# Operand splitting and block sums of a fast matrix product, moved from GpSimd to VectorE and put in another order

## The chip, the cores and the metric

The kernel runs on one core of a Trainium2 chip. Its engines are TensorE (PE in the rows, with its weight loads as PEld), VectorE (DVE), ScalarE (ACT), GpSimd (POOL) and SyncE (SP), which here issues the DMAs. The metric is the device time of one execution in microseconds, the median of three runs.

## The reference, cut to what matters

Two trunk layers act on 512 latent tokens and 128 context tokens, 640 rows of width 1024. Each layer has attention and then a SwiGLU feed-forward block of hidden width 2816. All is float32. What the change touches is the first half of the feed-forward block:

```
h = rms_norm(x, norm_ffn) * (1.0 + sc_f) + sh_f
gate, up = jnp.split(h @ w_gate_up, 2, axis=-1)
x = x + g_f * ((jax.nn.silu(gate) * up) @ w_down)
```

## The kernel before, in words

Every large matrix product is made of three matmuls. An operand is kept as a high part (the value rounded by a ScalarE copy to the fast matmul type) and a low part (the value minus its high part), and `prod` adds high·high, low·high and high·low in PSUM. `split` (L82) makes both parts: ScalarE writes the high one (L87), VectorE the low one (L88). Weights arrive by DMA as `raw` tiles, 1 MB each, two buffers, and are split into `whi` and `wlo`, four buffers of each.

In layer 1 (`FAST`) the gate and up products use the Strassen-Winograd scheme: the hidden activation, 1024 x 640, is cut into four blocks B11, B21 (first 320 tokens) and B12, B22 (last 320 tokens), each of four 128x320 tiles. From them come four sums, T3 = B22 - B12, T1 = B12 - B11, T2 = B22 - T1, T4 = B21 - T2. Seven products of a weight block with one of B11, B21, T2, T3, T1, T4, B22 replace eight. The weight blocks need sums too (`fast_prep`, L499): POOL makes four per raw tile, L506 to L509.

While these operands come into being, the first unit of 256 gate and up columns is done with the plain eight products (`plain_units`, L557). Its first half (`c == 0`) multiplies B11 and B21, its second half B12 and B22. Then come the fast products, seven for each of gate and up, in the order of their weight blocks A11, A12, S2, S3, S1, A22, S4, which multiply B11, B21, T2, T3, T1, T4, B22.

Before, the operands of the second half and all four sums are split by `cut` (L440): ScalarE writes the high part (L443), and POOL, not VectorE, the low part (L444). `fast_norm` (L446) does so for B12 and B22, `fast_sums` (L481) for T3, T1, T2, T4. The sums themselves run on VectorE (L487, L490, L492, L495, L496), all of them called between the two halves of `plain_units`. The weights of the next unit are split when `w_next` asks for them, which is after the second half in program order.

The program is not run in the order of the Python code: a scheduler orders each engine's queue by its own estimate of time, and each engine then works through its queue in order. An instruction that waits holds up all that is behind it on its engine. The names in the rows that follow: `lo4`-`lo7` are the tiles of B12; `k8`, `k9`, `q0`, `q1` those of B22; `q2`-`q5` T3; `q6`, `q7` and two `Q` tiles T1; a `Q` tile and three pieces of `V` T2; four pieces of `V` T4. `hi4`-`hi7` hold the unsplit B12 and B22 and later T1 and T2; three other `Q` tiles hold T3 and T4 before their split.

Of the kernel before, what the change touches and what calls it, by code (L numbers as in the profile page):

```python
# [11 lines left out]
F32 = mybir.dt.float32  # L12
F32R = mybir.dt.float32r
I32 = mybir.dt.int32
AF = mybir.ActivationFunctionType
ALU = mybir.AluOpType
# [5 lines left out]
KC = D // P  # L22
# [24 lines left out]
class Net:  # L47
# [389 lines left out]
        h = self.temp % 2  # L437
        return self.temps[self.temp // 2][:, h * HALF:(h + 1) * HALF]

    def cut(self, pair, src):  # L440

        hi, lo = pair
        self.nc.scalar.activation(hi, src, AF.Copy)  # L443
        self.nc.gpsimd.tensor_tensor(lo, src, hi.bitcast(F32), ALU.subtract)  # L444

    def fast_norm(self, state, half, rb):  # L446

        nc = self.nc
        v = nc.vector
        l, _, T, a = state  # L450
        g0, g1 = HALVES[half]
        segs = [(s, e, c) for s, e, c in ((g0, min(g1, DEC), 0), (DEC, g1, 1)) if s < e]

        def scaled(out, k):
            for s, e, c in segs:
                v.scalar_tensor_tensor(out[:, s - g0:e - g0], self.xT[k][:, s:e], a[:, k, c:c + 1],
                                       rb[:, s - g0:e - g0], ALU.mult, ALU.mult)

        n = KC // 2
        if half == 0:  # L460
            self.whole = {}
            for name, k0 in (("B11", 0), ("B21", n)):
                for i in range(n):
                    tmp = self.t([P, HALF], "P", bufs=3)
                    scaled(tmp, k0 + i)
                    self.split(*T[name][i], tmp, bias=self.m(l, 3, k0 + i, 0))
            return
        T["B12"] = []
        for i in range(n):
            tmp = self.t([P, 2, HALF], f"hi{n + i}")  # L470
            b12 = self.t([P, NT], f"lo{n + i}", F32R)
            T["B12"].append((b12[:, 0:HALF], b12[:, HALF:NT]))
            for j, k in enumerate((i, n + i)):
                scaled(tmp[:, j], k)
                for s, e, c in segs:
                    w = tmp[:, j, s - g0:e - g0]
                    nc.scalar.activation(w, w, AF.Identity, bias=self.m(l, 3, k, c))
                self.cut(T[("B12", "B22")[j]][i], tmp[:, j])
            self.whole[i] = tmp

    def fast_sums(self, T):  # L481

        v = self.nc.vector
        for i in range(KC // 2):
            b12, b22 = self.whole[i][:, 0], self.whole[i][:, 1]
            t3 = self.fast_temp()
            v.tensor_tensor(t3, b22, b12, ALU.subtract)  # L487
            self.cut(T["T3"][i], t3)
            for part in T["B11"][i]:
                v.tensor_tensor(b12, b12, part.bitcast(F32), ALU.subtract)  # L490
            self.cut(T["T1"][i], b12)
            v.tensor_tensor(b22, b22, b12, ALU.subtract)  # L492
            self.cut(T["T2"][i], b22)
            t4 = self.fast_temp()
            v.tensor_tensor(t4, T["B21"][i][0].bitcast(F32), b22, ALU.subtract)  # L495
            v.tensor_tensor(t4, t4, T["B21"][i][1].bitcast(F32), ALU.add)  # L496
            self.cut(T["T4"][i], t4)

    def fast_prep(self, raw, name):  # L499

# [56 lines left out]
    def plain_units(self, T, act):  # L557

        nc = self.nc
        g = [self.t([P, NT], "P", bufs=3) for _ in range(2)]
        n = KC // 2
        rows = [(k, b, i) for i in range(n) for k, b in ((i, 0), (n + i, 1))]
        w = [[self.w_next(1), self.w_next(1)], [self.w_next(1), self.w_next(0)]]
        for c, names in enumerate((("B11", "B21"), ("B12", "B22"))):
            if c == 0:
                rows = sorted(rows)
            else:  # L570
                self.fast_sums(T)
                rows = sorted(rows, key=lambda x: (x[2], x[0]))
            for r in range(2):
                s = self.S()
                o = g[r][:, c * HALF:(c + 1) * HALF]
                p = s[:, 0:HALF], s[:, 512:512 + HALF]
                for u in range(2):
                    hi, lo = w[r][u]
                    self.prod(p[u], [((hi[:, k], lo[:, k]), T[names[b]][i]) for k, b, i in rows])
                    if u == 0:  # L580
                        nc.scalar.activation(o, p[0], AF.Silu)
                nc.vector.tensor_tensor(o, p[1], o, ALU.mult)
        a = act(0), act(1)
        for r in range(2):
            self.split(*a[r], g[r])
# [751 lines left out]
```

## Time and profile before

| | |
|---|---|
| median of three runs | 1721.56 us (1719.19 to 1723.73) |
| profiled execution | 1722.35 us, of it 1720.3 us span |
| mean granted TensorE clock | 0.981 |
| TensorE busy | 1657.2 us, 96% of the span |
| VectorE, ScalarE, POOL busy | 1178.0, 671.5, 457.8 us |
| instructions of L443 and L444 | 24 each, between 1283 and 1315 us |

TensorE is busy nearly all the time, so what matters is each stretch in which it waits or runs at the lower of its two clock levels. PEclk in a row is the granted clock as a share of full speed: 1.00 is 2.4 GHz and 0.50 is 1.2 GHz. A duration in the timeline is that of the record; engines overlap the end of one instruction with the next, so the cost of one in a row of many is the distance between their starts.

### The profile page before, as it was taken

Reading aid. Unit: us, or ns where it says so; the run is one execution under the profiler, and the core shown is the slowest. Engines: PE = TensorE matmul, PEld = TensorE weight load, DVE = VectorE, ACT = ScalarE, POOL = GpSimd, SP = SyncE. Lnnn points to the kernel's source line nnn. Section 1 sums busy time; section 2 is a strip of 40 time slices with the busy share of each in tenths; the row PEclk is TensorE's granted clock in tenths of the full one; section 3 lists DMA queues with packets and bytes.
Section 4 is the critical chain, followed back from the end, with each engine's and each line's share of the span. In section 5 each row is a group of like instructions: output and inputs, shape, how many; then the busy total and the mean of one; then the engine's idle time right before and its main releaser. Section 6 shows DMA issues by size and latency. Waiting matters only on the chain.

```text
span 1720.3 us, 29417 instructions
## 1 busy us (share of the span) xinstructions
PE 1657.2 (96%) x11958; PEld 1577.8 (92%) x11958; DVE 1178.0 (68%) x1999; ACT 671.5 (39%) x1301; POOL 457.8 (27%) x402
## 2 busy tenths in 40 slices
PE   8989899999999999999999998999998999999999
PEld 6868878898999999999999998888987999999998
DVE  5686768878588987732257885678479944873772
ACT  4433376643422122212235524767344422441440
POOL 0242634410100000000003354453027613741440
PEclk8989999999999999999999999999998999999999
DMA  9343211144155555312122211112211222231222
GB/s 329 137 152 117 56 25 26 50 172 147 50 193 185 183 201 189 129 60 88 62 102 74 75 38 44 26 40 67 91 50 39 85 99 74 74 103 70 74 82 79
DMA packets 44263, 169.22 MB, mean 98 GB/s; under 512 B 5600, under 2 KB 8416, under 8 KB 32864
## 3 DMA queue, kind: packets, MB, share of 16 engines
q1 hardware_dynamic: 44128, 167.34, 29.2%
q8 instruction: 94, 1.54, 0.4%
q14 instruction: 41, 0.34, 0.1%
HBM read 152.90 MB, written 3.93 MB: 91 GB/s over the span
## 4 chain that ended last, share of the span: by engine, by line
PE 84%; DVE 7%; ACT 3%; DMA 2%; POOL 2%; issue 2%; SPq 0%; POOLq 0%; DVEq 0%; ACTq 0%
PE S L712 21%; PE S L711 21%; PE S L713 21%; PE S L1006 3%; PE mm L1027 3%; PE S L922 3%; PE S L923 2%; PE mm L1023 2%; PE S L237 2%; PE mm L711 1%; PE mm L712 1%; PE mm L713 1%; DMA Q<-in_w_mod 1%; DVE wlo L88 1%; DVE mx L942 1%
## 5 line engine op out<-in xcount | busy, mean ns | idle before, releaser
L87 ACT ACTIVATE whi<-raw 128x1024 fp32r<-128x1024 f32 (+2 forms) x272 | 224.6, 842 | 617.4 <-PE S L712 526.6
L88 DVE TENSOR_TENSOR wlo<-raw,whi 128x1024 fp32r<-128x1024 f32 (+2 forms) x272 | 302.4, 1127 | 100.2 <-ACT whi L87 95.9
L711 PE MATMUL S<-k,whi 128*128 128x256 f32 (+2 forms) x904 | 277.5, 310 | 9.3 <-ACT whi L87 8.0
L713 PE MATMUL S<-k,wlo 128*128 128x256 f32 (+2 forms) x904 | 279.2, 309 | 0.0
L712 PE MATMUL S<-lo,whi 128*128 128x256 f32 (+2 forms) x880 | 272.7, 310 | 0.0
L713 PE MATMUL S<-hi,wlo 128*128 128x384 f32 (+2 forms) x864 | 266.9, 310 | 0.0
L711 PE MATMUL S<-hi,whi 128*128 128x256 f32 (+2 forms) x864 | 266.2, 310 | 0.0
L712 PE MATMUL S<-q,whi 128*128 128x256 f32 (+2 forms) x832 | 257.6, 310 | 0.4 <-POOL q L444 0.4
L1158 DVE SCALAR_TENSOR_TENSOR x<-S,modT,x 128x128 f32<-128x128 f32 (+4 forms) x137 | 66.7, 525 | 195.5 <-PE S L713 195.4
L711 PEld LDWEIGHTS S<-k,whi 128*128 128x128 f32 x904 | 170.6, 190 | 10.9 <-ACT whi L87 8.3
L713 PEld LDWEIGHTS S<-k,wlo 128*128 128x128 f32 x904 | 171.0, 189 | 0.0
L712 PEld LDWEIGHTS S<-lo,whi 128*128 128x128 f32 x880 | 165.7, 188 | 1.7 <-issue 1.7
L713 PEld LDWEIGHTS S<-hi,wlo 128*128 128x128 f32 x864 | 162.5, 188 | 0.0
L711 PEld LDWEIGHTS S<-hi,whi 128*128 128x128 f32 x864 | 161.7, 188 | 0.8 <-issue 0.8
L712 PEld LDWEIGHTS S<-q,whi 128*128 128x128 f32 x832 | 157.0, 189 | 4.1 <-issue 3.4
L629 POOL TENSOR_TENSOR lo<-P,hi 128x640 fp32r<-128x640 f32 (+2 forms) x12 | 13.3, 1107 | 533.1 <-ACT hi L628 532.7
L317 DVE SCALAR_TENSOR_TENSOR Q<-V,cT,Q 128x512 f32<-128x512 f32 x224 | 152.8, 749 | 0.0
L711 PE MATMUL S<-whi,hi 128*128 128x256 f32 x512 | 146.8, 287 | 2.4 <-ACT Q L245 1.9
L942 DVE TENSOR_REDUCE mx<-S 128x1 f32<-128x768 f32 x128 | 119.5, 951 | 42.6 <-PE S L923 42.3
L713 PE MATMUL S<-whi,lo 128*128 128x256 f32 x512 | 145.9, 286 | 0.0
L712 PE MATMUL S<-wlo,hi 128*128 128x256 f32 x512 | 145.5, 284 | 0.0
L711 PEld LDWEIGHTS S<-whi,hi 128*128 128x128 f32 x512 | 97.5, 190 | 5.5 <-issue 2.5
(272 smaller groups left out, 3657.4 us busy)
## 6 DMA issues: line engine op xcount, KB each, us to landing
raw<-in_w_gate_up SPq DMA_DIRECT2D x44, 1024.0 KB, 4.8
V<-in_w_mod SPq DMA_DIRECT2D x64, 512.0 KB, 3.9
raw<-in_w_in SPq DMA_DIRECT2D x16, 1024.0 KB, 4.9
raw<-in_w_down SPq DMA_DIRECT2D x16, 1024.0 KB, 5.0
Q<-in_w_mod SPq DMA_DIRECT2D x32, 256.0 KB, 3.7
raw<-in_w_out SPq DMA_DIRECT2D x8, 1024.0 KB, 4.8
raw<-in_w_down SPq DMA_DIRECT2D x8, 768.0 KB, 4.2
raw<-raw SPq DMA_DIRECT2D x40, 128.0 KB, 2.2
```

What stands on the lines that cost most here:

```text
L87: nc.scalar.activation(hi, src, AF.Copy)
L88: nc.vector.tensor_tensor(lo, src, hi.bitcast(F32), ALU.subtract)
L237: nc.tensor.matmul(o, lhsT=l_[k][:, c], rhs=r_[:, w], start=k == 0 and i == 0, stop=k == KC - 1 and i == 2)
L317: ins = nc.vector.scalar_tensor_tensor(a, v, self.cT[:, k, c:c + 1], a, ALU.mult, ALU.add)
L711: self.nc.tensor.matmul(out, lhsT=lh, rhs=rh, start=(i == 0), stop=False)
L712: self.nc.tensor.matmul(out, lhsT=lh, rhs=rl, start=False, stop=False)
L713: self.nc.tensor.matmul(out, lhsT=ll, rhs=rh, start=False, stop=(i == n - 1))
L922: nc.tensor.matmul(out, lhsT=Q[j][:, cols], rhs=keys[:, k0:k0 + n], start=True, stop=False)
L942: nc.vector.tensor_reduce(mx, s[:, 0:n], AX.X, ALU.max, negate=True)
L1006: nc.tensor.transpose(ps[:, i * P:(i + 1) * P], p[:, i * P:(i + 1) * P], self.ident)
L1027: nc.tensor.matmul(o[64 * j:64 * j + 64], lhsT=self.V[:, v, 512 + 64 * j:576 + 64 * j], rhs=pts[j][:, i * P:(i + 1) * P], start=first, sto ...
L1158: self.nc.vector.scalar_tensor_tensor(x[:, s:e], src[:, s - a:e - a], self.m(l, which, mb, c), x[:, s:e], ALU.mult, ALU.add)
```

## The change

`cut` is gone. Wherever it stood, `split` stands: the low parts of B12, B22, T1, T2, T3 and T4, 24 of 128x320, are now VectorE's (L88). `fast_sums` is a generator in three parts. Its first part makes T3, T1 and T2 and splits T2 and T3; its second splits T1 and makes and splits T4. The first is called between the two halves of `plain_units` as before, the second after both, and between them the split of the next unit's first weights is called (`w_prep(self.pos + 3)`: A11, A12 and S2). Nothing else is edited.

```diff
-    def cut(self, pair, src):
-
-        hi, lo = pair
-        self.nc.scalar.activation(hi, src, AF.Copy)
-        self.nc.gpsimd.tensor_tensor(lo, src, hi.bitcast(F32), ALU.subtract)
-
...
-                self.cut(T[("B12", "B22")[j]][i], tmp[:, j])
+                self.split(*T[("B12", "B22")[j]][i], tmp[:, j])
             self.whole[i] = tmp
 
     def fast_sums(self, T):
 
         v = self.nc.vector
-        for i in range(KC // 2):
+        n = KC // 2
+        for i in range(n):
+
             b12, b22 = self.whole[i][:, 0], self.whole[i][:, 1]
             t3 = self.fast_temp()
             v.tensor_tensor(t3, b22, b12, ALU.subtract)
-            self.cut(T["T3"][i], t3)
             for part in T["B11"][i]:
                 v.tensor_tensor(b12, b12, part.bitcast(F32), ALU.subtract)
-            self.cut(T["T1"][i], b12)
             v.tensor_tensor(b22, b22, b12, ALU.subtract)
-            self.cut(T["T2"][i], b22)
+            self.split(*T["T2"][i], b22)
+            self.split(*T["T3"][i], t3)
+        yield
+        for i in range(n):
+            self.split(*T["T1"][i], self.whole[i][:, 0])
+        for i in range(n):
             t4 = self.fast_temp()
-            v.tensor_tensor(t4, T["B21"][i][0].bitcast(F32), b22, ALU.subtract)
+            v.tensor_tensor(t4, T["B21"][i][0].bitcast(F32), self.whole[i][:, 1], ALU.subtract)
             v.tensor_tensor(t4, t4, T["B21"][i][1].bitcast(F32), ALU.add)
-            self.cut(T["T4"][i], t4)
+            self.split(*T["T4"][i], t4)
+        yield
...
-                self.fast_sums(T)
+                sums = self.fast_sums(T)
+                next(sums)
                 rows = sorted(rows, key=lambda x: (x[2], x[0]))
...
                 nc.vector.tensor_tensor(o, p[1], o, ALU.mult)
+        self.w_prep(self.pos + 3)
+        next(sums)
         a = act(0), act(1)
```

What the scheduler makes of it, first on ScalarE, where the high part of the first fast weight stands. Before it is `whi_13609`, behind high parts of T1, T2 and T4 (`q7`, `V`, `Q`):

```order
L443 ACTIVATE q3_12986<-Q_12995 128x320
L443 ACTIVATE q4_12987<-Q_12996 128x320
L443 ACTIVATE V_12972<-Q_12995 128x320
L443 ACTIVATE q5_12988<-Q_12994 128x320
L443 ACTIVATE q7_12990<-hi5_13284 128x320
L443 ACTIVATE V_12972<-hi5_13284 128x320
L443 ACTIVATE Q_12991<-hi6_13298 128x320
L443 ACTIVATE V_12972<-hi6_13298 128x320
L87 ACTIVATE whi_13609<-raw_13607 128x512 x2
```

In the changed kernel it is `whi_13574` (its L582 is the Silu of the plain unit, L581 before):

```order
L87 ACTIVATE q3_12986<-Q_12995 128x320
L87 ACTIVATE q4_12987<-Q_12995 128x320
L87 ACTIVATE q5_12988<-Q_12996 128x320
L87 ACTIVATE whi_13574<-raw_13572 128x512 x2
L582 ACTIVATE P_13326<-S_13470 128x320
L87 ACTIVATE whi_13585<-raw_13572 128x512
L582 ACTIVATE P_13327<-S_13521 128x320
L87 ACTIVATE V_12972<-Q_12996 128x320
L87 ACTIVATE q7_12990<-hi5_13284 128x320
```

The weight's high part now stands behind T3 alone (`q3` to `q5`), and five high parts that were ahead of it are behind it. On VectorE the end of the sums reads before as follows (the low parts are on POOL; `wlo` is a low part of a weight, L582 the product of gate and up):

```order
L88 TENSOR_TENSOR wlo_13610<-raw_13607,whi_13609 128x512
L496 TENSOR_TENSOR Q_12994<-Q_12994,k6_12979 128x320
L88 TENSOR_TENSOR wlo_13610<-raw_13607,whi_13609 128x512
L88 TENSOR_TENSOR wlo_13621<-raw_13607,whi_13620 128x512
L495 TENSOR_TENSOR Q_12995<-k7_12980,hi7_13312 128x320
L496 TENSOR_TENSOR Q_12995<-Q_12995,k7_12980 128x320
L582 TENSOR_TENSOR P_13326<-S_13494,P_13326 128x320
```

and in the changed kernel, where the three last low parts of T4 are the rows `V_12972<-Q`:

```order
L495 TENSOR_TENSOR Q_12995<-Q_12995,k7_12980 128x320
L88 TENSOR_TENSOR V_12972<-Q_12994,V_12972 128x320
L88 TENSOR_TENSOR wlo_13696<-raw_13676,whi_13695 128x512
L88 TENSOR_TENSOR V_12972<-Q_12994,V_12972 128x320
L532 TENSOR_TENSOR Q_12995<-S_13659,Q_12995 128x320
L88 TENSOR_TENSOR wlo_13737<-raw_13676,whi_13736 128x512
L88 TENSOR_TENSOR wlo_13737<-PT_13711,whi_13736 128x512
L88 TENSOR_TENSOR V_12972<-Q_12995,V_12972 128x320
```

T4's last low part now comes behind weight splits of the second fast unit. TensorE of the changed kernel uses it here (the product of A22 with T4, in `S_13694`):

```order
L714 MATMUL S_13694<-V_12972,whi_13626 128x320
L714 MATMUL mm_13864<-k8_12981,whi_13769 128x320
L715 MATMUL mm_13864<-k8_12981,whi_13769 128x320
L715 MATMUL S_13694<-V_12972,whi_13626 128x320
L716 MATMUL S_13694<-V_12972,wlo_13627 128x320
L714 MATMUL S_13788<-Q_12993,whi_13695 128x320
```

The fourth row is the one that waits for that low part, and everything behind it on TensorE waits with it. POOL loses its 24 instructions and keeps the weight sums, in the same order.

## Rows read from the trace of the kernel before

**Rows 1.** The page: busy time of the engines, then the chain's shares by engine.
```profile
PE 1657.2 (96%) x11958; PEld 1577.8 (92%) x11958; DVE 1178.0 (68%) x1999; ACT 671.5 (39%) x1301; POOL 457.8 (27%) x402
PE 84%; DVE 7%; ACT 3%; DMA 2%; POOL 2%; issue 2%; SPq 0%; POOLq 0%; DVEq 0%; ACTq 0%
```

**Rows 2.** Stages: length, busy us (instructions) by engine, granted clock, DMA share, GB/s.
```profile
1290.00:1300.00 10.00, 6.34 (x42) 5.82 (x40) 9.96 (x10) 4.01 (x10) 10.00 (x10) 0.94 0.00 1
1300.00:1310.00 10.00, 5.21 (x21) 4.87 (x22) 10.00 (x13) 5.13 (x12) 7.77 (x8) 0.54 0.01 2
```

**Rows 3.** Timeline of TensorE: start us, us, operation, [idle before, releaser].
```profile
1288.90 0.31 PE L711 MATMUL S<-lo,whi 128*128 128x320 f32 x1
1289.05 0.31 PE L712 MATMUL S<-lo,whi 128*128 128x320 f32 x1
...
1295.93 0.41 PE L712 MATMUL S<-q,whi 128*128 128x320 f32 x1 [0.44 <-POOL q L444]
1296.18 0.31 PE L713 MATMUL S<-q,wlo 128*128 128x320 f32 x1
...
1304.79 0.63 PE L711 MATMUL S<-k,whi 128*128 128x320 f32 x1 [8.01 <-ACT whi L87]
...
1308.73 0.47 PE L713 MATMUL S<-k,wlo 128*128 128x320 f32 x1
1309.00 0.37 PE L711 MATMUL S<-lo,whi 128*128 128x320 f32 x1
```

**Rows 4.** Timeline of ScalarE at the end of that stall.
```profile
1303.75 0.47 ACT L443 ACTIVATE V<-hi 128x320 fp32r<-128x320 f32 x1 [1.31 <-DVE hi L492]
1304.12 1.13 ACT L87 ACTIVATE whi<-raw 128x512 fp32r<-128x512 f32 x2
1305.16 0.42 ACT L581 ACTIVATE P<-S 128x320 f32<-128x320 f32 x1
```

**Rows 5.** Timeline of VectorE, from the first sum on.
```profile
1286.69 0.48 DVE L487 TENSOR_TENSOR Q<-hi 128x320 f32<-128x320 f32 x1
...
1302.57 1.14 DVE L492 TENSOR_TENSOR hi<-hi 128x320 f32<-128x320 f32 x1
...
1305.79 0.48 DVE L495 TENSOR_TENSOR Q<-k,hi 128x320 f32<-128x320 f32 x1
1306.19 0.48 DVE L496 TENSOR_TENSOR Q<-Q,k 128x320 f32<-128x320 f32 x1
...
1312.17 1.06 DVE L496 TENSOR_TENSOR Q<-Q,k 128x320 f32<-128x320 f32 x1
...
1317.72 1.28 DVE L88 TENSOR_TENSOR wlo<-raw,whi 128x512 fp32r<-128x512 f32 x2
1318.92 0.81 DVE L88 TENSOR_TENSOR lo<-P,hi 128x640 fp32r<-128x640 f32 x1
...
1322.81 2.27 DVE L88 TENSOR_TENSOR wlo<-raw,whi 128x512 fp32r<-128x512 f32 x2
```

**Rows 6.** Timeline of POOL in the same stretch.
```profile
1303.33 1.10 POOL L444 TENSOR_TENSOR Q<-hi,Q 128x320 fp32r<-128x320 f32 x1
1304.40 1.12 POOL L444 TENSOR_TENSOR V<-hi,V 128x320 fp32r<-128x320 f32 x1
...
1322.63 1.29 POOL L509 TENSOR_TENSOR raw<-raw 128x512 f32<-128x512 f32 x1 [1.74 <-DVE wlo L88]
```

**Rows 7.** Stages around two earlier stalls, columns as in rows 2.
```profile
1030.00:1032.00 2.00, 0.75 (x7) 0.51 (x5) 0.57 (x1) 0.39 (x1) 1.94 (x2) 1.00 0.02 5
1032.00:1034.00 2.00, 1.16 (x10) 0.93 (x9) 0.00 (x0) 0.00 (x0) 2.00 (x3) 1.00 0.00 0
1266.00:1268.00 2.00, 0.77 (x7) 0.59 (x5) 2.00 (x6) 2.00 (x5) 0.00 (x0) 1.00 0.90 360
1268.00:1270.00 2.00, 0.70 (x7) 0.48 (x5) 2.00 (x4) 0.53 (x2) 0.30 (x1) 1.00 0.32 135
...
1272.00:1274.00 2.00, 2.00 (x10) 2.00 (x8) 2.00 (x5) 0.61 (x2) 0.55 (x1) 0.50 0.63 266
```

## The prediction

> **What bounds the kernel now.** I read the page first: TensorE is busy 96% of the span and 84% of the chain [rows 1], so an edit pays only where TensorE waits or runs slow. The view by stages finds the place: from 1290 to 1310 us TensorE is busy 6.34 and 5.21 of 10 us, while VectorE shows 9.96 and 10.00 and POOL 10.00 and 7.77 [rows 2]. This is just where L443 and L444 work. The timeline of TensorE shows the loss itself [rows 3]. From 1288.90 it takes 48 matmuls of the plain unit's second half, 0.147 us apart, and would be through at 1295.94. It waits 0.44 us for a POOL low part, starts the next instruction, the first fast product with weight A11, only at 1304.79 after an idle 8.01 us, and then runs at 1.2 GHz: the granted clock is 0.54 in that stretch [rows 2] and matmuls stand 0.27 us apart until 1309.00 [rows 3]. The matmul at 1309.00 is the 15th from the one at 1304.79, so 14 distances of 0.147, 2.06 us, would have done. It would have started at 1298.00: TensorE loses 11.0 us here, and after it no view shows it waiting again before the last stores.
>
> The timeline of ScalarE says why the stall ends so late [rows 4]: A11's high part starts at 1304.12, as soon as the high part ahead of it in the queue (T2's third tile) is done, and that one waited for VectorE's sum (L492), which ends at 1303.71 [rows 5]. VectorE is not slow by its own work. Its 128x320 operations take 1.14 us while POOL works, and stand 0.40 us apart at 1305.79 and 1306.19 in a gap of POOL's [rows 5]. POOL's own stand 1.07 apart [rows 6]. The two engines take turns.
>
> The page SBUF — State Buffer of the Trainium skill (Who interferes with whom) states the same: a VectorE instruction with two SBUF inputs and a GpSimd instruction that reads SBUF exclude each other for a whole instruction. [...]
>
> **The change, part by part.**
>
> *Low parts on VectorE.* POOL loses 24 instructions and is then idle until it may overwrite the first raw tile, that is until A11's low part exists. VectorE gains 24 of a kind that no row shows: 128x320, all operands in SBUF. Nearest are the sums of that shape: 0.40 us alone, 1.07 in turns [rows 5, 6]. I take 0.40, since POOL has nothing to do there.
>
> *A11's split earlier.* In the changed queue of ScalarE A11 stands right behind T3. VectorE's last T3 sum is the 19th instruction from 1286.69, so it ends at about 1286.69 + 19 x 0.40 = 1294.3. But A11's high part overwrites the weight of the plain unit's first product, which TensorE reads until about 1295.65 (the 45th of the 48 matmuls starts at 1295.35 and takes 0.31). With a high part 0.62 us (record, two in 1.13 [rows 4]) A11 is ready at 1296.3, and TensorE, through at 1295.94, waits 0.45 us in place of 8.01. No low part is late before that: the last one of B22 is the 15th VectorE instruction, 1292.7, and is wanted at 1295.3.
>
> *What is late next.* Three things.
> - The rest of the plain unit accumulates in a PSUM tile that the Silu (0.42 us [rows 4]) must first read, and the Silu stands behind A11's and A12's high parts: TensorE waits another 0.5 us and is there at 1297.4.
> - T2's second low part is VectorE's 47th instruction (41 of 0.40, 6 weight low parts of 0.60, by the pair in 1.28 [rows 5]: 20.0 us), with two weight sums of POOL in between. Such a sum costs VectorE about 1.0 us (a pair of weight low parts takes 2.27 beside POOL's L509 and 1.28 alone [rows 5, 6]). It lands near 1309.2; TensorE, 76 matmuls on, is there at 1308.6. With a PSUM buffer that is freed 0.25 us late behind it, 0.8 us.
> - T4's last low part is the 68th: 54 of 0.40, 12 of 0.60, 2 of 0.73 (the 640 wide one, 0.81 less the overlap of 0.08 [rows 5]) make 30.3 us, with its own end 1317.0. On top come POOL's sums for three raw tiles, six instructions at 1.0, and some tenths of waits for ScalarE: 1323.4. TensorE, 154 matmuls (22.6 us) after 1297.4, plus the waits above, is there at 1321.0, so it waits 2.4 us. This is the largest term and the least known. If no POOL instruction falls on it the wait is 0; with eight at POOL's full 1.3 us [rows 6] T4 lands at 1327.4 and the wait is 6.4.
>
> Each restart after a wait costs about 0.1 us (0.25 in place of 0.15 at 1295.93 [rows 3]), five of them 0.5. Loads don't move: SyncE's queue is unchanged, and the third raw tile is asked for somewhat earlier.
>
> **Sum.** New losses: 0.45 + 0.5 + 0.8 + 2.4 + 0.5 = 4.65 us in place of 11.0, a gain of 6.35. Behind that TensorE has no idle time that could take it back. From the profiled execution's own 1722.35 us (the span 1720.3 and 2.05 around it) it makes 1716.0. That execution lies 0.8 above the median of 1721.56, so I forecast **1715.2**.
>
> **The rivals.**
> - *The clock falls all the same.* The new waits at T4, some 2.4 us within about 4 us, are broken up by matmuls. Around 1030 us TensorE was busy 0.75 and 1.16 of two 2 us stretches and the clock stayed at 1.00; after 0.77 and 0.70 at 1266 it went to 0.50 (1272) [rows 7]. Mine lies nearer the first. If it falls, some 15 matmuls at 0.27 cost 1.9 us more, as after 1304.79: 1717.1. Chance 0.2.
> - *T4 is in time*, because POOL's sums fall where VectorE waits anyway or are fewer. The 2.4 us and one restart are saved: 1712.7. Chance 0.12.
> - *The gain goes back to VectorE.* Eight turns with POOL at 1.3 us, T4 at 1327.4, and a longer stall with the clock at 0.50 after it: 4.0 and 1.9 more, so the time is 1721.1, no change. For it: VectorE is now the fullest engine of the stretch. Against it: POOL has only weight sums there. Chance 0.13.
> - *Slower: VectorE is the bound whatever POOL does.* If the turns come from VectorE itself, each of the 24 added low parts costs it 1.07 us. The last sum, done at 1313.2 now [rows 5], moves by 25.7 us to about 1339, TensorE waits 18 us for T4 in place of 2.4, and the time is 1731. It decides once the 68 instructions take over 0.63 us each on average (T4 beyond 1329.7); my sum has 0.54. Against it are the 0.40 us in POOL's gap [rows 5]. [...] Chance 0.06.
>
> **How the numbers follow.** My forecast has 0.49. Its own range is 1714 to 1717, by half a microsecond either way in the clockless terms and one in T4's landing. With the rivals the range is 1711.8 to 1718.9: it holds the forecast, the fallen clock and the case in time, and leaves out the slower case and most of the no-change one. About 0.3%, 5.2 us, is what a measurement of this kernel can tell from no change, so faster means below 1716.4. The forecast is there with 0.85 of its 0.49, the fallen clock with a quarter of its 0.2 and T4 in time wholly, together 0.58. Slower, beyond 1726.7, has most of the last rival, 0.05. The rest, 0.37, is no change.
>
> **What would show it.** In the profile after: L88's low parts of 128x320 about 0.40 us apart between 1287 and 1298 with POOL idle (if they stand 1.07 apart, the slower rival is right); A11's high part at about 1295.7 behind TensorE's matmul and not behind VectorE; the wait of 8.0 us for `whi` replaced by one under 1 us; granted clock 1.00 from 1296 to 1310; then two or so waits of 1 to 2.5 us near 1320 for the low part L88 of `V` (T4). The forecast is wrong if a wait over 3 us stands there, if the clock drops after it, or if a wait for `wlo` in the following fast unit shows that VectorE has not caught up.

## The result, and the profile after

The changed kernel takes 1711.38 us (median of five runs), beside 1719.52 us of six runs of the kernel before on the same chip: 0.995 of it, with an interval of 0.9932 to 0.9967, so 5.7 to 11.7 us faster. A sixth run, disturbed throughout (2568.56 us at a mean granted clock of 0.578), is left out. A second comparison gave 1713.04 us and 0.9966 (0.9955 to 0.9978). The forecast was 1715.2 within 1711.8 to 1718.9, so the direction was right, and the first median lies 0.4 us below the range. The profiled execution took 1714.41 us, with a span of 1712.6.

The page after, the lines of [rows 1]: POOL has 24 instructions fewer, VectorE 24 more, and the chain has 2 points more of TensorE.

```profile
PE 1655.6 (97%) x11958; PEld 1575.6 (92%) x11958; DVE 1173.0 (68%) x2023; ACT 670.4 (39%) x1301; POOL 436.7 (25%) x378
PE 86%; DVE 6%; DMA 3%; ACT 2%; POOL 2%; issue 1%; SPq 0%; DVEq 0%; POOLq 0%; ACTq 0%
```

The stages of the changed kernel, columns as in [rows 2]:

```profile
1290.00:1300.00 10.00, 9.42 (x63) 8.91 (x62) 10.00 (x25) 5.09 (x12) 2.34 (x1) 1.00 0.01 2
1300.00:1310.00 10.00, 9.83 (x65) 9.29 (x64) 9.65 (x18) 6.73 (x14) 3.77 (x2) 1.00 0.00 0
1310.00:1320.00 10.00, 9.33 (x63) 8.81 (x61) 10.00 (x14) 4.38 (x10) 7.56 (x4) 1.00 0.32 107
1320.00:1330.00 10.00, 9.01 (x59) 8.64 (x60) 9.97 (x19) 5.11 (x10) 4.94 (x4) 1.00 0.29 105
```

TensorE is busy 9.42 and 9.83 where it had 6.34 and 5.21, at a granted clock of 1.00 throughout. VectorE is as full as before, but with 25 and 18 instructions in place of 10 and 13: it does more in the same time. What TensorE still loses stands in its timeline (columns as in [rows 3]):

```profile
1294.73 0.30 PE L716 MATMUL S<-q,wlo 128*128 128x320 f32 x1
1295.33 0.41 PE L714 MATMUL S<-k,whi 128*128 128x320 f32 x1 [0.29 <-ACT whi L87]
...
1296.17 0.41 PE L714 MATMUL S<-lo,whi 128*128 128x320 f32 x1 [0.29 <-ACT P L582]
...
1307.67 0.42 PE L715 MATMUL S<-V,whi 128*128 128x320 f32 x1
...
1308.48 0.42 PE L714 MATMUL S<-q,whi 128*128 128x320 f32 x1
...
1318.96 0.42 PE L715 MATMUL S<-V,whi 128*128 128x320 f32 x1 [0.67 <-DVE V L88]
...
1321.97 0.41 PE L715 MATMUL S<-V,whi 128*128 128x320 f32 x1 [0.99 <-DVE V L88]
```

The 8.01 us before A11's product are 0.29. The two rows without brackets (1307.67, where T2's second low part is waited for, and 1308.48, the PSUM buffer behind it) are read from the starts: 0.39 and 0.40 us after their predecessors, at 1307.28 and 1308.08, in place of 0.147. ScalarE now does A11's and A12's high parts behind TensorE's last reading of the buffer, as the releaser says, and not behind VectorE (compare [rows 4]):

```profile
1294.64 1.15 ACT L87 ACTIVATE whi<-raw 128x512 fp32r<-128x512 f32 x2 [0.78 <-PE S L715]
1295.70 0.42 ACT L582 ACTIVATE P<-S 128x320 f32<-128x320 f32 x1
```

VectorE's timeline, from the first low part to T4's last, with its longest rows (compare [rows 5]):

```profile
1285.64 0.48 DVE L88 TENSOR_TENSOR lo<-hi,lo 128x320 fp32r<-128x320 f32 x1
1286.04 0.49 DVE L483 TENSOR_TENSOR Q<-hi 128x320 f32<-128x320 f32 x1
...
1292.07 1.29 DVE L483 TENSOR_TENSOR Q<-hi 128x320 f32<-128x320 f32 x3
...
1301.11 0.49 DVE L583 TENSOR_TENSOR P<-S,P 128x320 f32<-128x320 f32 x1
1301.51 1.18 DVE L486 TENSOR_TENSOR hi<-hi 128x320 f32<-128x320 f32 x1
1303.04 1.36 DVE L88 TENSOR_TENSOR wlo<-raw,whi 128x512 fp32r<-128x512 f32 x1 [0.35 <-ACT whi L87]
...
1312.49 0.48 DVE L532 TENSOR_TENSOR P<-S,Q 128x320 f32<-128x320 f32 x1
1312.89 1.18 DVE L495 TENSOR_TENSOR Q<-Q,k 128x320 f32<-128x320 f32 x1
1314.00 1.92 DVE L88 TENSOR_TENSOR lo<-P,hi 128x640 fp32r<-128x640 f32 x1
1315.84 1.57 DVE L495 TENSOR_TENSOR Q<-Q,k 128x320 f32<-128x320 f32 x1
1317.33 1.57 DVE L88 TENSOR_TENSOR V<-Q,V 128x320 fp32r<-128x320 f32 x1
...
1321.43 0.48 DVE L88 TENSOR_TENSOR V<-Q,V 128x320 fp32r<-128x320 f32 x1
```

and POOL's in the same stretch, which is weight sums alone (compare [rows 6]):

```profile
1297.66 4.69 POOL L508 TENSOR_TENSOR raw<-PT,raw 128x512 f32<-128x512 f32 x1 [22.92 <-DVE wlo L88]
1302.42 1.43 POOL L509 TENSOR_TENSOR raw<-raw 128x512 f32<-128x512 f32 x1
1310.84 2.88 POOL L508 TENSOR_TENSOR raw<-PT,raw 128x512 f32<-128x512 f32 x1 [6.99 <-DVE wlo L88]
1313.80 1.43 POOL L509 TENSOR_TENSOR raw<-raw 128x512 f32<-128x512 f32 x1
1315.19 1.88 POOL L506 TENSOR_TENSOR PT<-raw 128x512 f32<-128x512 f32 x1
1317.14 1.41 POOL L507 TENSOR_TENSOR raw<-raw 128x512 f32<-128x512 f32 x1
```

Low parts stand 0.40 us apart while POOL is idle, and even beside its first sum of 4.69 us. Six rows from 1301.51 to 1317.33 are long, 5.4 us together over what such instructions take elsewhere (0.48, with 512 elements 0.68, with 640 0.81): they hold T4 back.

**Where in the program the time went.** Three marks cut the span: the first load of the stage's weights (`raw<-in_w_gate_up` at 1225.02 before), the first scaling of the second half (L450, in the kernel before L456, at 1282.01), and the first load of that name behind those of `in_w_down` (1406.38 before). In the changed kernel they are:

```profile
1222.93 125.62 SPq L683 DMA_DIRECT2D raw<-in_w_gate_up  x8
1280.96 4.76 DVE L450 SCALAR_TENSOR_TENSOR hi<-x,A,mm 128x192 f32<-128x192 f32 x16 [2.17 <-PE mm L402]
1398.67 12.57 SPq L683 DMA_DIRECT2D raw<-in_w_gate_up  x2
```

A is from the first mark to the second, B from the second to the third, where all of the change's work lies. Every kernel below takes 276.82 or 276.83 us from the third mark to the store of the output.

| profile | first mark | A | B |
|---|---|---|---|
| before | 1225.02 | 56.99 | 124.37 |
| before, again | 1224.70 | 56.92 | 125.02 |
| changed | 1222.93 | 58.03 | 117.71 |
| changed, again | 1219.00 | 58.07 | 117.71 |
| e1 low parts on VectorE, old order | 1221.28 | 56.93 | 117.70 |
| e2 new order, low parts on POOL | 1222.39 | 56.84 | 124.10 |
| e3 changed, no early weights | 1225.10 | 56.99 | 117.71 |
| e7 first 16 low parts on POOL | 1221.88 | 56.95 | 122.29 |
| e6 T1 and T4 low parts on POOL | 1220.82 | 58.10 | 120.26 |
| e9 the same, PSUM reads between | 1221.52 | 58.13 | 119.06 |
| e4 weight sums on VectorE | 1220.43 | 58.59 | 114.87 |
| e4, repeated | 1224.46 | 58.59 | 114.85 |
| e5 the same, two units alone | 1222.15 | 58.61 | 116.12 |
| e8 e4 in the old order | 1225.75 | 58.60 | 116.30 |

In e4, e5 and e8 TensorE has 20 more of its matmuls ahead of the second mark, which moves work from B into A; there the two are to be added. B repeats to 0.01 us in the changed kernel and in e3. It is 6.66 us shorter than in the first profile of before and 7.31 shorter than in the second, where TensorE stayed at 1.2 GHz behind the stall until 1310.18 and not 1309.00, which made up the 0.65 us between the two. The time to the first mark is anything from 1219.0 to 1225.8, with the same queues up to there. The profile's 7.94 us are these 6.66, plus 2.09 ahead of the first mark, less 1.04 in A, where the clock fell to 0.50 twice and not once, and 0.2 around the span and by rounding.

### The profile page after: what moved, and what is told of

The parts are those of the page before. It is cut to its first block, busy times and chain, and to the rows that moved or that the text cites. A ratio compares the mean times of both kernels' runs of the same rounds, so it can differ in the third digit from the quotient of the medians.

```text
span 1712.6 us, 29412 instructions
## 1 busy us (share of the span) xinstructions
PE 1655.6 (97%) x11958; PEld 1575.6 (92%) x11958; DVE 1173.0 (68%) x2023; ACT 670.4 (39%) x1301; POOL 436.7 (25%) x378
## 4 chain that ended last, share of the span: by engine, by line
PE 86%; DVE 6%; DMA 3%; ACT 2%; POOL 2%; issue 1%; SPq 0%; DVEq 0%; POOLq 0%; ACTq 0%
PE S L715 21%; PE S L714 21%; PE S L716 21%; PE mm L1030 3%; PE S L1009 3%; PE S L925 3%; PE S L926 2%; PE mm L1026 2%; PE S L237 2%; PE mm L714 1%; PE mm L716 1%; PE mm L715 1%; DVE wlo L88 1%; DMA Q<-in_w_mod 1%; DMA raw<-in_w_in 1%
## 5 line engine op out<-in xcount | busy, mean ns | idle before, releaser
L88 DVE TENSOR_TENSOR wlo<-raw,whi 128x1024 fp32r<-128x1024 f32 (+2 forms) x272 | 293.7, 1093 | 96.6 <-ACT whi L87 92.1
```

The lines of the kernel that those rows point to most:

```text
L88: nc.vector.tensor_tensor(lo, src, hi.bitcast(F32), ALU.subtract)
```

## The experiments

**Engine or order?** My theory was that the engine does it; the rival, that the order does, with the weights asked for early.

e1, the old order of sums and weights, with all low parts on VectorE:

```diff
 def cut(self, pair, src):
-    hi, lo = pair
-    self.nc.scalar.activation(hi, src, AF.Copy)
-    self.nc.gpsimd.tensor_tensor(lo, src, hi.bitcast(F32), ALU.subtract)
+    self.split(*pair, src)
```

> The low parts of all 24 operands go to VectorE, but the sums are written in the old order, all of them between the two halves, and the weights are not asked for early. Theory A (the engine does it: without GpSimd's turns the sums reach ScalarE at VectorE's own pace, and the weights' high parts, which stand behind them in ScalarE's queue, come in time): about as fast as the changed kernel, 5 to 9 us faster than before, the wait for the weight's high part below 1 us. Rival O (the order does it, the weights' high parts ahead of T1 and T4): the wait of 8 us stays at 5 us or more, and the time is within 2 us of before.

Measured: 1714.98 us, 0.9967 (0.9954 to 0.9979), B 117.70: the whole gain.

e2, the new order, with every `split` of B12, B22 and T1 to T4 turned back into `cut`:

> The sums in the new order, in two parts, with the next unit's weights asked for between them, but the low parts of all 24 operands on GpSimd as before. Theory A (engine): as before within 2 us, with a wait of 6 to 9 us for the weight's high part and the clock at 0.50 behind it. Rival O (order): 5 us or more faster than before, the wait below 2 us.

Measured: 1719.59 us, 0.9999 (0.999 to 1.0009). The waits of TensorE from 1280 to 1330 us, in us (total, times, longest), first e2's:

```profile
PE S L720 <- ACT whi L87: 8.0, 1, 8.0
PE S L721 <- POOL q L444: 0.4, 1, 0.4
```

and e1's:

```profile
PE S L710 <- DVE V L88: 1.1, 2, 0.6
...
PE S L709 <- ACT whi L87: 0.3, 1, 0.3
```

The old wait is there, to a tenth, in e2 and gone in e1. The order as written does nothing for it alone. ScalarE's timelines say how the engine comes in, first e2's, then e1's:

```profile
1300.97 0.47 ACT L443 ACTIVATE V<-hi 128x320 fp32r<-128x320 f32 x1 [1.67 <-DVE hi L492]
1301.35 1.13 ACT L87 ACTIVATE whi<-raw 128x512 fp32r<-128x512 f32 x2
```

```profile
1291.88 1.15 ACT L87 ACTIVATE whi<-raw 128x512 fp32r<-128x512 f32 x2 [0.71 <-PE S L710]
```

In e2 A11's high part stands behind T2's third tile, as before; in e1 the scheduler put it ahead of that tile, as in the changed kernel, and it waits for TensorE alone. VectorE is not sooner with that tile's sum: it ends 17.0 us after VectorE's first sum before (1303.71) and in e2, 17.0 us after the first low part in the changed kernel (1302.69) and 16.65 in e1. It is VectorE's 39th instruction in the changed kernel, where it was the 18th, so VectorE does more up to there in the same time. So in turns with POOL the sums were too late for a weight that stood behind them, and what took the wait away is the weight's earlier place on ScalarE. No run moves that place alone, and why the scheduler puts it there once the low parts are VectorE's is not shown.

e3, the changed kernel less one line:

```diff
-        self.w_prep(self.pos + 3)
         next(sums)
```

> The changed kernel without the line that asks for the next unit's weights between the two parts of the sums. The queues of VectorE and ScalarE differ from the changed kernel's in 4 rows each, GpSimd's in none. Theory A (that line does nothing here): from the first scaling of the second half to the same load at the end of the stage 117.7 us again, to 0.5 us, and the changed kernel's time to 2 us. Rival O (it brings the high parts forward): the wait for the weight's high part is back with 2 us or more. As a further profile of the same code up to 1281 us it also tells whether the second fall of the clock there (58.0 and not 57.0 us from the load to the first scaling) comes with VectorE's low parts in the new order, as in the changed kernel's two profiles, or by chance.

Measured: 1712.84 us, 0.9951 (0.9939 to 0.9964), B 117.71, the wait for `whi` 0.3 us. The line does nothing here; by the names of their tiles the instructions of B stand in the same order as in the changed kernel on every engine.

**Which low parts?** e7 puts B12, B22, T2 and T3 on POOL (`cut`), T1 and T4 on VectorE.

> The changed kernel, with the low parts of B12, B22, T2 and T3 (16 of the 24) on GpSimd, those of T1 and T4 on VectorE. Theory A (it is the pace of the sums behind GpSimd's turns that makes ScalarE late at the weights): VectorE and GpSimd alternate at 1.07 us from the first low part on, the wait for the weight's high part comes back, with 3 to 8 us, and most of the gain goes: within 3 us of before. Rival T (T1 and T4, the last in ScalarE's queue ahead of the weights, make the wait): a wait below 2 us, and 4 us or more faster than before.

Measured: 1717.68 us, 0.9994 (0.9979 to 1.0009), B 122.29, and in the view of waits:

```profile
PE S L720 <- ACT whi L87: 6.1, 1, 6.1
```

So the wait comes with the first 16 low parts on POOL, and T1's and T4's on VectorE don't help: the time of rival T falls. Pace alone is not shown by it. VectorE's last sums of T3,

```profile
1287.54 3.34 DVE L489 TENSOR_TENSOR Q<-hi 128x320 f32<-128x320 f32 x3
```

end 7.4 us after its first sum (1283.51), and in the changed kernel 7.7 us after its first low part. Right behind T3, A11's high part could be as early here as there. It starts at 1298.28, because high parts of T4, T1 and T2 stand ahead of it on ScalarE, the last of them (T2's second tile) at 1297.90.

e6 is the reverse, T1 and T4 on POOL:

```diff
-            self.split(*T["T1"][i], self.whole[i][:, 0])
+            self.cut(T["T1"][i], self.whole[i][:, 0])
...
-            self.split(*T["T4"][i], t4)
+            self.cut(T["T4"][i], t4)
```

> The changed kernel, with the low parts of T1 and T4 (8 of the 24) on GpSimd, those of B12, B22, T2 and T3 on VectorE. Theory A (a low part on GpSimd costs VectorE a turn of 0.67 us and saves it one instruction of 0.40 us, so VectorE is 8 x 0.27 = 2.2 us later at T4): no wait of more than 1 us for a weight's high part, but the waits for T4's low parts grow from 1.7 to 3 to 6 us; 1 to 4 us slower than the changed kernel. Rival N (the number of VectorE's instructions sets T4): VectorE is 3.2 us earlier, the waits for T4 vanish, 1 to 2 us faster than the changed kernel.

Measured: 1716.54 us, 0.9983 (0.9973 to 0.9992), B 120.26, 2.55 us longer than the changed kernel's. The size is what theory A gave, and rival N, which had it faster, falls. But theory A's mechanism is not what the waits show:

```profile
PE mm L720 <- ACT whi L87: 1.8, 1, 1.8
PE S L721 <- DVE V L88: 1.0, 1, 1.0
```

TensorE does not wait for T4, whose low parts are POOL's (L444) here. The `V` of VectorE is T2's second low part (0.96 us), and the product into `mm` is that of S4 with B22, so 1.78 us go to S4's high part. The timeline of POOL in e6 shows why, its first low part:

```profile
1288.28 10.80 POOL L444 TENSOR_TENSOR q<-hi,q 128x320 fp32r<-128x320 f32 x1 [15.57 <-ACT q L443]
```

An instruction of 0.88 us took 10.80, and the weight sums stood behind it. VectorE in that time kept its 0.40 us; the theory of turns does not give this. Its timeline where POOL's instruction ends (1299.08):

```profile
1297.45 0.89 DVE L492 TENSOR_TENSOR hi<-hi 128x320 f32<-128x320 f32 x2
1298.26 0.49 DVE L589 TENSOR_TENSOR P<-S,P 128x320 f32<-128x320 f32 x1
1298.66 0.78 DVE L492 TENSOR_TENSOR hi<-hi 128x320 f32<-128x320 f32 x1
```

L589 is the first instruction since 1288.28 that reads PSUM (S). The same stands in the changed kernel: the sums of 4.69 and 2.88 us end 1.2 us after L583 (1301.11) and L532 (1312.49), which read S.

e9 tests this: e6, with such a reading after each low part of T3:

```diff
             self.split(*T["T3"][i], t3)
...
+            v.scalar_tensor_tensor(junk, T["T3"][i][1][:, 0:3].bitcast(F32), a[:, 0, 0:1], rb[:, 0:3], ALU.mult, ALU.mult)
```

> T1 and T4 on GpSimd as in the run before of that kind, and after each low part of T3 a VectorE instruction of 128x3 that reads PSUM, whose result nobody uses. There GpSimd's first low part took 10.80 us beside 27 VectorE instructions that started 0.40 us or 0.60 us apart, and ended 0.8 us after the first of them that read PSUM. Theory P (GpSimd's instruction gets in only where VectorE's next one reads PSUM, or where VectorE waits): that low part ends 0.8 to 1.5 us after the first such instruction, which stands some 3 rows behind its start, so after 2 to 3.5 us in all, and from there VectorE and GpSimd alternate at about 1.07 us. Rival W (it gets in where VectorE itself had to wait for another engine, as it did near there): the added instructions change nothing, 9 us or more again.

Measured: POOL's low parts in e9,

```profile
1289.01 2.17 POOL L444 TENSOR_TENSOR q<-hi,q 128x320 fp32r<-128x320 f32 x1 [15.58 <-ACT q L443]
1296.13 2.57 POOL L444 TENSOR_TENSOR V<-Q,V 128x320 fp32r<-128x320 f32 x1 [4.96 <-ACT V L443]
```

and VectorE's added instructions around them:

```profile
1290.35 0.21 DVE L498 SCALAR_TENSOR_TENSOR junk<-q,A,mm 128x3 f32<-128x3 f32 x1
...
1297.88 0.20 DVE L498 SCALAR_TENSOR_TENSOR junk<-q,A,mm 128x3 f32<-128x3 f32 x1
```

Each of the two ends 0.82 or 0.83 us after such an instruction starts, so one that reads PSUM lets POOL in, and W falls. That POOL gets in only there, as theory P has it, does not hold. In e7 it got in at once between two VectorE instructions that read SBUF alone and stand 0.40 us apart:

```profile
1298.19 0.48 DVE L492 TENSOR_TENSOR hi<-hi 128x320 f32<-128x320 f32 x1
1298.45 0.95 POOL L444 TENSOR_TENSOR V<-hi,V 128x320 fp32r<-128x320 f32 x1 [2.54 <-ACT V L443]
1298.60 1.16 DVE L88 TENSOR_TENSOR q<-hi,q 128x320 fp32r<-128x320 f32 x1
```

What makes POOL starve in one place and not in the other stays open. B is 119.06, 1.20 less than e6's; in time (1713.9 us, 0.9959, 0.9944 to 0.9974) the two are hard to tell apart.

**What is left before T4.** e4 puts the weight sums on VectorE:

```diff
-            nc.gpsimd.tensor_tensor(self.s1, a21, a22, ALU.add)
+            nc.vector.tensor_tensor(self.s1, a21, a22, ALU.add)
```

and so for the other three.

> The changed kernel, with the four sums of each unit's weights (128x512) on VectorE and not on GpSimd. Theory A (what is left before T4 is GpSimd's turns: six weight sums between 1297 and 1319 us make VectorE wait 5.6 us, four more between 1267 and 1275 us make it wait about 4 us, while on VectorE each would take the 0.60 us between the starts of two low parts of 512): T4's last low part 3.2 us earlier (5.6 less 4 x 0.60), so its waits of 1.7 us go, and 1 to 2 us come off the first half's scaling: 2 to 4 us faster than the changed kernel. Rival N (T4 is late by the number of VectorE's instructions): eight more at 0.60 us, 2.4 us of them ahead of T4 and 2.4 us in the first half, 2 to 5 us slower than the changed kernel.

> All weight sums on VectorE, once more. Theory A: again 7 to 9 us faster than before (0.995 of it), 1 to 3 us faster than the changed kernel's 0.9966; from load to load 173.5 us, to 0.5 us, but for the clock's falls (about 1 us each). Rival (the first comparison was luck): within 1 us of the changed kernel.

Measured: 1711.59 us, 0.9952 (0.9939 to 0.9964), and in the repeat 1713.64 us, 0.995 (0.9937 to 0.9964). The timeline of VectorE in e4, at the end of T4 (the first low part is at 1284.10):

```profile
1314.90 0.67 DVE L509 TENSOR_TENSOR raw<-raw 128x512 f32<-128x512 f32 x1
...
1316.10 0.47 DVE L88 TENSOR_TENSOR V<-Q,V 128x320 fp32r<-128x320 f32 x1
```

T4 is done 32.5 us after the first low part, 3.8 us sooner than in the changed kernel (36.3), and its waits are gone. So more instructions on VectorE, and less time: rival N falls. But A and B together are 173.45 us (the mean of the two), only 1.25 less than e3's 174.70 (which has as many falls of the clock) and not 2 to 4. By time alone e4 can't be told from the changed kernel, which gave 0.995, 0.9966 and, as e3, 0.9951. It is the version I would keep, on the profile's word.

e5 does so for the first two units alone (`eng = nc.vector if self.summed <= 2 else nc.gpsimd`).

> The changed kernel, with the weight sums of the first two units alone on VectorE, the later ones on GpSimd as before. Theory A (only the turns before T4 cost TensorE anything; later it is 100% busy in either case): the same time as with all sums on VectorE, to 1 us, 1 to 3 us faster than the changed kernel. Rival L (the turns of the later units matter too): the changed kernel's time to 1 us, slower than with all sums on VectorE by 1 to 2 us.

Measured: 1712.45 us, 0.9958 (0.9944 to 0.9971), A and B 174.73: 1.3 more than e4, of which 0.94 us is a wait for a high part at 1383.70. Theory A missed this; nearer is rival L.

e8 is e1 with the weight sums on VectorE.

> Low parts and weight sums all on VectorE, the sums of the token blocks written in the old order (no parts, no early weights). Theory A (the engine decides, not the order): the same time as with the new order and the weight sums on VectorE, to 1.5 us, 0.994 to 0.996 of the kernel before. Rival O: 2 us or more slower than that.

Measured: 1714.31 us, 0.996 (0.9947 to 0.9972), A and B 174.90, 1.45 more than e4; TensorE waits 1.9 us for a weight's low part at 1312.38. Within the bound I had set, but here the new order helps a little.

**The two kernels again.**

> The changed kernel once more, nothing edited. Theory A (the gain lies in the stretch from the 48 plain matmuls to the last product of the first unit, where the profile gave 6.65 us from the first scaling of the second half on, and the 2.1 us of lead that it had already at 1225 us are the clock of one execution): the median of the differences is 6 to 9 us, the one long wait for a weight's high part is below 0.5 us again, the waits for the low parts of T4 add up to 1.5 to 2 us again, and the lead before 1225 us is another one than 2.1 us. Rival B (the lead of 2.1 us belongs to the change): it stands at 1225 us again, to within 0.3 us.

> The kernel before once more, nothing edited, for a second profile of it. Its clock and its lead tell what of the differences between two profiles is the execution's. Theory A: from the first scaling of the second half to the same load at the end of the stage it takes the same 124.4 us as in the first profile, to 0.3 us, while the time up to 1225 us comes out another by 1 to 6 us, and the clock falls in the first half once or twice. Rival B (the second fall of the clock in the first half belongs to the changed kernel alone, which showed it in both of its profiles): here it falls once, and from the load at 1225 us to the first scaling of the second half it takes 57.0 us and not 58.0.

Measured: the changed kernel 0.9966, as above, with T4's two waits of 1.7 us together and the wait for `whi` 0.3; the kernel before 1721.36 us, 1.0006 of itself (0.9994 to 1.0019), with B at 125.02 and not within 0.3 of 124.4, as said above. The time to its first mark, 1224.70, differs by 0.3 us and not by 1 to 6. The lead of 2.1 us at the first mark is not the change's: the second profile had 6.0, and e3 none. The second fall of the clock in A came in both profiles of the changed kernel and in e6 and e9, not in e3, which runs the same instructions in the same order, nor in the other nine. So it is not tied to those instructions alone, and what sets it stays open. Where it comes, the gain over A and B together is 5.6 us and not 6.66.

## Why the prediction missed its range

- *What bounds it: right.* The loss between the plain unit and A11's product, counted in the starts of TensorE over 0.147, was 11.1 us (I had 11.0). I named two causes, A11's place on ScalarE behind T2's third tile and sums 1.07 us apart in turns with POOL. That it took both is argued: 18 instructions at 0.40 us would have ended near 1294, in time. The place is what changed, since the sum came no sooner. I put it down to the new order as well; e1 shows that the engine brings it by itself.
- *Low parts at 0.40 us: right.* The slower rival (1.07 whatever POOL does) is out.
- *A11 and the Silu: right.* 0.45 and 0.5 forecast, 0.45 and 0.45 by the starts at 1295.33 and 1296.17.
- *T2: over-sized.* 0.8 forecast, 0.24 and 0.25 measured. POOL's first sum of 4.69 us did not slow VectorE until 1301.51.
- *T4: right, by 0.3.* 2.4 forecast, 0.83, 0.16 and 1.15 measured, so the rival of T4 in time is out. T4's last low part came 36.3 us after the first instruction (36.7 forecast). POOL's six weight sums cost VectorE 5.4 us, where I had 6.0.
- *Restarts: under-sized.* Eight of 0.1, not five.
- *The sum.* 4.65 forecast, 4.3 measured, with the restarts and T2 in part making up for each other; the gain 6.35 forecast, 6.66 by B (7.31 from the second profile of before). No wait of over 3 us came, and the clock stayed at 1.00 after T4, so the rivals of the fallen clock and of a gain given back to VectorE are out too.
- *The step that failed: the basis, "That execution lies 0.8 above the median of 1721.56, so I forecast 1715.2", and the range around it.* The basis was the median of three runs, and the range held only the unknowns of the stage. The medians of before are 1719.52 (6 runs), 1719.88 (17), 1720.62 (10) and 1720.93 (27): 0.6 to 2.0 lower. The time up to the first mark, which the change does not touch, varies by 6.75 us over 14 profiles, and the second fall of the clock adds 1.1 or not. 1719.52 less 6.66 is 1712.9; the remaining 1.5 us to 1711.38 are within that variation, and the second comparison's 1713.04 and e3's 1712.84 lie in the range. So the mechanism and the sum stand, and on which side of 1711.8 a median falls is partly chance.

## What to carry to other kernels

Where a queue is in order, look for what stands ahead of the late instruction and for the engine whose pace feeds that: ScalarE was late at the weights because they stood behind sums that VectorE, in turns with POOL, finished late. Moving the low parts to the fuller engine did not slow VectorE on the way to T2's third sum, since a turn cost 0.67 us and the instruction 0.40, and it did not bring that sum sooner either; the gain came with the weights' new place. So read the compiled queues of every engine anew after such an edit. Compare two profiles by marks of their own on either side of the change, and put the spread of what lies ahead of them, measured on more than three runs, into the range.

## What the hardware showed

- POOL beside a VectorE without gaps may not get its turn: a 0.88 us instruction took 10.80 us, until VectorE ran one that reads PSUM (e6), and 2.17 with such a one put in (e9). It is not always so (0.95 us in e7). Once POOL's next instruction is ready as the last one ends, the two alternate (1.07 us apart in [rows 6]). The Trainium skill, SBUF — State Buffer (Who interferes with whom), has it that a VectorE instruction with at most one SBUF input, outside the 2-port performance modes, does not contend with GpSimd. The traces agree: `P<-S,P` has one, and it is where POOL got in.
- The clock stayed at 1.00 in the changed kernel through T4's waits, with TensorE busy 3.33 and 3.01 us of the two stretches of 4 us from 1316. In e6 it was busy 1.80 us from 1304 to 1308, and from there to 1314 the granted clock was 0.50 (1.2 GHz).
